# Two projection groups as one seven-product block multiplication, with weight sums made by accumulating DMAs

## The chip, the cores and the metric

The kernel runs on one core of a Trainium2 chip, as one program. The metric is device time in microseconds from launch to end, lower is better. The engines named here are TensorE (PE: matmuls; PEld is its weight load), VectorE (DVE), ScalarE (ACT), GpSimd (POOL) and SyncE (SP). SP does no arithmetic; its queue issues nearly all DMAs, in program order, and a DMA that has to wait there holds all that stand behind it. POOL issues the DMAs that add to their destination.

## What is computed

A decoder block over 1024 tokens of width 1024: an RMS norm with adaptive scale and shift gives `h`, one wide projection of `h` feeds a retention mixer and a dilated sliding-window attention in three groups of four heads, both are gated and merged, and a squared-ReLU MLP follows. The part that matters here is the projection, and of it the attention values of the three groups:

```python
proj = h @ w_in
parts = jnp.split(proj, IN_OFFSETS, axis=-1)
...
for gi, (win, dil) in enumerate(ATT_GROUPS):
    aq, ak, av = parts[4 + 3 * gi], parts[5 + 3 * gi], parts[6 + 3 * gi]
```

Each `av` is `h` (1024 x 1024) times a weight of 1024 x 512.

## The kernel before

All matmuls are made of three: an operand is split into a high part in the fast float32 format (`hi`, a cast on ACT) and a low part (`lo = x - hi`, a subtraction on DVE), and a product is lo x hi + hi x lo + hi x hi, accumulated in PSUM (`mm3`, L197). `h` lies in SBUF transposed, as eight pairs `hh[k]`, `hl[k]` of 128 channels by 1024 tokens. A matmul is 128 x 128 by 128 x 512; PSUM has eight banks of 128 x 512.

The order of the instructions on each engine is the order in which the program writes them; the program sets it by hand, and semaphores only make an engine wait. So an instruction that waits holds what is behind it on its engine. Tiles come from pools: `raw` (three slots, L144) for weights as loaded, `wh` and `wl` (three slots each) for their parts, and `x` (26 slots, `x4`, L332) for nearly all else in this stage. A new tile waits until the last reader of the tile that had its slot is done.

**Startup and the first value group** (`av_first`, L779). `h` is made channel block by channel block: DVE scales `xt[k]`, ACT makes `hh[k]`, DVE `hl[k]`. As soon as block k is there, PE multiplies it with the weight rows k of group 0 (`av_k`, L746), for eight token blocks at once, in eight banks. At k = 4 `bias_out` (L436) puts the attention bias into DRAM: three times one small write and four broadcast writes that wait for it. After k = 7 ACT copies the eight banks to SBUF tiles `avo`, and SP writes them to `va_d`.

**The second and the third group** (`av_step`, L854) go the same way, now with `h` complete: for each of the eight k and eight token blocks three matmuls, in all 2 x 8 x 8 x 3 = 384, and again eight copies and eight writes at the end of each group. The weights of a pair of k are one load of 128 x 1024; the planner `Steps` (L55) issues the loads as slots of `raw` come free, and splits a weight ahead of its step.

**Sums of h** (`sums_of_h`, L824). The stages that follow (queries, keys, gates, retention values) use Winograd's form of Strassen's algorithm: the tokens are cut in halves and the channels in even and odd blocks, and seven products of half size replace eight. Their left operands are blocks of `h` and the sums t1 to t4, each a set of four tiles `xat` (t4 takes the place of half of `hh` and `hl`, whose contents are saved to DRAM in `h12_d` before). In the kernel before t1, t3 and t2 are made within the second group, and t4 at the head of `queries_keys` (L954). One set is four times a DVE operation, a cast on ACT and a subtraction on DVE.

**Queries and keys** (`queries_keys`). The class `Blocks` (L220) runs the seven products for each pair of 128 output columns. Its `prep` makes the sums of the weights on DVE and splits them, some products ahead; `post` takes the banks out (L280 is a copy on ACT, L284 and L285 are subtractions on DVE). Four operands of the first pair are prepared within the third value group.

**Sums in DRAM.** For later stages, weight sums are made in DRAM: `copy_block` copies a block and `quarter_sums` (L548) adds others to it with DMAs that POOL issues (L552; L556 and L558 are plain copies among them), each of 512 KB. These begin with `queries_keys`. `VPLAN` lists the seven products of the retention values: which left operand, which sign of the weight, and which of three bank groups (a, b, c) they are accumulated in.

Of the kernel before, what the change touches and what calls it, by code (L numbers as in the profile page):

```python
# [11 lines left out]
F32 = mybir.dt.float32  # L12
F32R = mybir.dt.float32r
AF = mybir.ActivationFunctionType
# [120 lines left out]
def block_kernel(ctx, tc, io, stop=None, dbg=None):  # L135
# [3 lines left out]
    def fv(t):  # L139
        return t.bitcast(F32)  # L140
# [638 lines left out]
    def av_first(kk):  # L779

        def body(ahead, w):
            for k in (2 * kk, 2 * kk + 1):
                if k == 0:
                    for j, rb in enumerate(first["rb"]):
                        nc.scalar.copy(rb1[:, 512 * j:512 * j + 512], rb)
                if k % 2 == 0:
                    ahead(1)
                if k + 1 < NK:
                    h1_mods(k + 1)
                    h1_scale(k + 1)  # L790
# [24 lines left out]
        return body  # L815
# [35 lines left out]
            low = lo, r, hi  # L851
        nc.vector.tensor_sub(low[0], low[1], fv(low[2]))

    def av_step(g, kk):  # L854
        def body(w):
            if (g, kk) == (1, 0):
                for m in range(4):
                    nc.sync.dma_start(h12_d[m][:, 0], fv(hh[2 * m][:, 512:]))
                    nc.sync.dma_start(h12_d[m][:, 1], fv(hl[2 * m][:, 512:]))
                sh = mods[:, SH1:SH1 + NK].rearrange("p (m j) -> p m j", j=2)  # L860
                nc.vector.tensor_sub(dsh1, sh[:, :, 0], sh[:, :, 1])
            for k in (2 * kk, 2 * kk + 1):
                av_k(g, k, w)
            if g == 1 and kk < 3:
                sums_of_h(("t1", "t3", "t2")[kk])
            if (g, kk) == (1, 3):
                a_load(0, 1)
                a_load(0, 2)
            if (g, kk) == (2, 1):
                BA.prep((0, "11"), (0, "s1"))  # L870
            if (g, kk) == (2, 2):
                a_load(1, 1)
                a_load(1, 2)
                BA.prep((0, "s3"), (0, "s2"))
        return body
# [224 lines left out]

    for kk in range(4):
        steps.add(av_first(kk), [(io["w_av"][kk], split_first)], manual=True)
    for g in (1, 2):
        for kk in range(4):
            steps.add(av_step(g, kk), [(io["w_av"][4 * g + kk], split_first if (g, kk) == (1, 0) else split_w)])
    steps.mark()
    steps.add(queries_keys, manual=True)

    later_mods = [G1 + k for k in range(NK)] + [SH2 + k for k in range(NK)] + \
# [1343 lines left out]
```

## Time and profile before

| | us |
|---|---|
| three timed runs | 2242.38, 2243.01, 2244.39 (median 2243.01) |
| profiled execution, first to last instruction | 2248.9 |
| its mean granted TensorE clock | 0.993 of full |
| first matmul of the second value group | 72.50 |
| first matmul of queries and keys | 159.54 |

The profiled execution has no time of its own beside its span of 2248.9 us. All times below are from its start. A line of the page's or the trace's groups reads: program line, engine, operation, output <- inputs, shapes, count | busy time in us, mean ns of one | idle time of the engine before them and what ended it. A line in order of time reads: start, length, engine, line, operation, output <- inputs, count, and in square brackets the idle time before it and what released it. The table of stages gives for each stretch the busy time and the number of instructions of each engine, the granted clock, the share of time that the DMA engines were busy and GB/s. In the lists of DMAs the last number is the median time from issue to landing.

### The profile page before, as it was taken

How to read it: one execution, taken by the hardware profiler on the slowest of the kernel's cores; microseconds unless marked ns; L12 is line 12 of the kernel's file. 1: busy time of each engine (PE TensorE's matmuls, PEld its weight loads, DVE VectorE, ACT ScalarE, POOL GpSimd, SP SyncE). 2: the span in 40 equal slices, each digit the busy share in tenths (PEclk: the TensorE clock that was granted, in tenths of full speed). 3: DMA queues.
4: the chain of work that ended last, by engine and by line, in shares of the span. 5: the costliest groups of instructions: out<-in, count | busy, mean ns of one | idle time of the engine just before them, and what ended most of it. 6: DMA issues, size and time to landing. Idle time of an engine off the chain costs nothing.

```text
span 2248.9 us, 27131 instructions
## 1 busy us (share of the span) xinstructions
PE 2183.6 (97%) x10130; PEld 1808.0 (80%) x10130; DVE 1455.3 (65%) x2285; ACT 908.6 (40%) x1665; POOL 145.6 (6%) x168
## 2 busy tenths in 40 slices
PE   7999999999999999999999999999999999999998
PEld 5887888887877888887788788888778888888887
DVE  6527777753548778853554554576866665787845
ACT  4323333223334445534634633434454445533412
POOL 0001111000011122100000000002100000000003
PEclk9999999999999999999999999999999999999999
DMA  9648999625775556549723345645134443745322
GB/s 361 197 145 277 289 284 287 198 93 178 246 271 169 168 181 206 191 165 241 207 78 94 105 178 210 247 156 178 61 136 155 155 155 145 266 151 169 122 85 76
DMA packets 154371, 408.93 MB, mean 182 GB/s; under 512 B 27062, under 2 KB 54973, under 8 KB 149822
## 3 DMA queue, kind: packets, MB, share of 16 engines
q1 hardware_dynamic: 148542, 363.14, 46.3%
q0 software_dynamic: 5696, 44.04, 8.2%
q8 instruction: 80, 1.31, 0.2%
q14 instruction: 53, 0.43, 0.1%
HBM read 316.27 MB, written 156.13 MB: 210 GB/s over the span
## 4 chain that ended last, share of the span: by engine, by line
PE 47%; DVE 5%; ACT 2%; DMA 2%; issue 1%; SPq 0%; POOL 0%; POOLq 0%; DVEq 0%; ACTq 0%
PE fp L201 4%; PE fp L203 4%; PE fp L205 4%; PE f2a L203 2%; PE f2a L205 2%; PE f2a L201 2%; PE ak L201 1%; PE ak L203 1%; PE ak L205 1%; PE wo L201 1%; PE wo L205 1%; PE wo L203 1%; PE roa L203 1%; PE roa L201 1%; PE roa L205 1%
## 5 line engine op out<-in xcount | busy, mean ns | idle before, releaser
L201 PE MATMUL qap<-hh,qaw 128*128 128x512 f32 x216 | 84.3, 390 | 3.9 <-ACT qat L280 2.2
L205 PE MATMUL qap<-hh,qaw 128*128 128x512 f32 x216 | 84.1, 389 | 0.0
L203 PE MATMUL qap<-hl,qaw 128*128 128x512 f32 x216 | 84.0, 389 | 0.0
L614 POOL TENSOR_TENSOR j<-qk,j 128x512 fp32r<-128x512 f32 x32 | 43.4, 1356 | 470.2 <-ACT j L613 470.2
L1912 ACT ACTIVATE a<-a 128x512 f32<-128x512 f32 x48 | 30.3, 631 | 79.1 <-DVE a L1911 79.1
L1266 ACT ACTIVATE P<-P,ng 128x128 f32<-128x128 f32 (+1 forms) x96 | 41.9, 438 | 41.8 <-DVE ng L1263 41.8
L1809 POOL TENSOR_TENSOR accnf<-accnf,sqnf 128x256 f32<-128x256 f32 (+1 forms) x18 | 16.6, 922 | 619.0 <-ACT sqnf L1808 619.0
L258 DVE TENSOR_TENSOR fw<-w1r,fw 128x512 fp32r<-128x512 f32 x48 | 33.0, 688 | 36.3 <-ACT fw L248 36.3
L2098 ACT CAST w2h<-w2s 128x512 fp32r<-128x512 f32 x36 | 22.4, 621 | 77.6 <-DVE w2s L2136 75.3
L201 PEld LDWEIGHTS qap<-hh,qaw 128*128 128x128 f32 x216 | 40.5, 188 | 13.2 <-ACT qat L280 2.6
L201 PE MATMUL fp<-h2h,fw 128*128 128x512 f32 x128 | 50.0, 390 | 0.0
L203 PE MATMUL fp<-h2l,fw 128*128 128x512 f32 x128 | 49.8, 389 | 0.0
L205 PE MATMUL fp<-h2h,fw 128*128 128x512 f32 x128 | 49.8, 389 | 0.0
L201 PE MATMUL roa<-rh,rwl 128*128 128x512 f32 x128 | 49.8, 389 | 0.0
L203 PE MATMUL roa<-rl,rwh 128*128 128x512 f32 x128 | 49.8, 389 | 0.0
L205 PE MATMUL roa<-rh,rwh 128*128 128x512 f32 x128 | 49.8, 389 | 0.0
L636 ACT COPY sm<-sT 128x128 f32<-128x128 f32 x32 | 8.5, 267 | 101.8 <-PE sT L627 100.1
L1647 DVE TENSOR_TENSOR rwl<-rwl,rwh 128x1024 fp32r<-128x1024 f32 x25 | 30.2, 1221 | 29.0 <-ACT rwh L1677 29.0
L1809 POOL TENSOR_TENSOR accn<-accn,sqn 128x512 f32<-128x512 f32 x12 | 15.5, 1296 | 491.8 <-ACT sqn L1808 491.8
L205 PEld LDWEIGHTS qap<-hh,qaw 128*128 128x128 f32 x216 | 40.5, 188 | 8.4
L203 PEld LDWEIGHTS qap<-hl,qaw 128*128 128x128 f32 x216 | 40.5, 188 | 8.3
L1204 DVE SCALAR_TENSOR_TENSOR ql<-raw,qh 128x1024 fp32r<-128x1024 f32 x12 | 14.7, 1224 | 47.6 <-ACT qh L1203 47.6
(3081 smaller groups left out, 7216.7 us busy)
## 6 DMA issues: line engine op xcount, KB each, us to landing
v<-vd SPq DMA_DIRECT2D x32, 512.0 KB, 5.4
raw<-in_w_ada_dram SPq DMA_DIRECT2D x32, 512.0 KB, 4.9
w1r<-in_w_ff_dram SPq DMA_DIRECT2D x32, 512.0 KB, 5.1
vd<-vo SPq DMA_DIRECT2D x24, 512.0 KB, 6.4
yt<-y POOLq DMA_DIRECT2D x6, 2048.0 KB, 15.0
xsd<-as SPq DMA_DIRECT2D x24, 512.0 KB, 2.7
w2r<-in_w_ff2s_dram SPq DMA_DIRECT2D x24, 512.0 KB, 7.1
em<-in_w_ada_dram SPq DMA_DIRECT2D x16, 512.0 KB, 10.2
```

The lines of the kernel that those rows point to most:

```text
L201: nc.tensor.matmul(o, wl, xh, start=first, stop=False, skip_group_check=skip)
L203: nc.tensor.matmul(o, wh, xl, start=False, stop=False, skip_group_check=skip)
L205: nc.tensor.matmul(o, wh, xh, start=False, stop=last, skip_group_check=skip)
L258: nc.vector.tensor_sub(t[:, 512:], src, fv(t[:, :512]))
L614: nc.gpsimd.tensor_sub(t[:, 1], src, fv(t[:, 0]))
L636: nc.scalar.copy(sm, ps[:, :C])
L1204: nc.vector.scalar_tensor_tensor(lo, raw, QSCALE, fv(hi), op0=ALU.mult, op1=ALU.subtract)
L1266: nc.scalar.activation(v, v, AF.Exp, bias=ng[:, blk:blk + 1], accum_out=st[:, g, blk, 2 + a:3 + a])
L1647: nc.vector.tensor_sub(lo, fv(lo), fv(hi))
L1809: (nc.vector if f == 7 else nc.gpsimd).tensor_add(G["acc", key], G["acc", key], sq)
L1912: nc.scalar.activation(o, o, AF.Relu)
L2098: nc.scalar.copy(hi, src)
```

## The change

The second and third group together are `h` (1024 x 1024) times a weight of 1024 x 1024. The change makes this one block multiplication with seven products, by the plan `VPLAN`: blocks 11, 12, s1, s2, s3, 22, s4, each of four quarters m, four token blocks p and three matmuls, 48 in all, so 336 for the stage (`av_blocks`, `avb_mm`). The first digit of a weight block is the group, the second the parity of the channel block.

- *Weights.* The four loads of group 1 (`avb_load`: abr0 to abr3) serve blocks 11 and 12 together. They are issued on SP at k = 4 (abr0, behind `bias_out`), k = 5 (abr2), k = 6 (abr1) and after k = 7 (abr3, behind the writes of `avo`), and are split (`avb_split`) before k = 6 and before k = 7 (abr0, abr1) and after the first quarter of block 11 (abr2, abr3). The planner no longer loads these groups.
- *Sums of weights.* s1 = 21 + 22, s2 = s1 + 11 and s4 = s2 + 12 are made one after the other in the same two `raw` tiles: a load by SP, then DMAs of POOL that add from DRAM into SBUF, the next one issued as soon as the tile has been split (`avb_sum`). s3 = 21 + 11 is a load and one addition in `x` tiles, 22 a plain load (`avb_fetch`). Each has two halves j; each addition moves 512 KB in rows of 2 KB. That is eight accumulating DMAs.
- *Banks.* `avb_post` takes a block's banks out during the first quarter of the next: blocks 11, s2, s1 and 22 by ACT, 12, s3 and s4 by an addition or subtraction on DVE. The results go to `va_d` as before.
- *Sums of h.* t1 is made after k = 7, behind the copies of the first group; t3 after the second quarter of block 11, t2 after the third of block 12, t4 after the second of s1. `queries_keys` no longer makes t4. The saves to `h12_d` move ahead of the loads of cos, sin and decay.
- *Operands of the first pair of queries and keys* are loaded in block s2 and prepared in blocks s3 and 22.

```diff
+                if k in (6, 7):
+                    avb_split(k - 6)
                 av_k(0, k, w)
...
                 if k == 4:
                     for g in range(3):
                         bias_out(g)
+                    avb_load(0)
+                if k == 5:
+                    avb_load(2)
+                if k == 6:
+                    avb_load(1)
+                    for j in range(2):
+                        avb_sum(j, "s1")
                 if k == NK - 1:
-                    ahead(1)
-                    if first["lows"]:
-                        first["lows"].pop(0)()
+                    avb_load(3)
+                    for m in range(4):
+                        nc.sync.dma_start(h12_d[m][:, 0], fv(hh[2 * m][:, 512:]))
+                        nc.sync.dma_start(h12_d[m][:, 1], fv(hl[2 * m][:, 512:]))
+                    sh = mods[:, SH1:SH1 + NK].rearrange("p (m j) -> p m j", j=2)
+                    nc.vector.tensor_sub(dsh1, sh[:, :, 0], sh[:, :, 1])
+                    sums_of_h("t1")
                     nc.sync.dma_start(cs, io["cossin"])
                     nc.sync.dma_start(decay, io["decay"])
...
+    def avb_tile(n, part, name):
+        if n in (2, 6) or n > 11:
+            return x4(name, F32R)
+        return whl.tile([P, 1024], F32R, tag="w" + part, name=name)
+
+    def avb_load(m):
+        AB["w", m] = x4(f"abr{m}")
+        nc.sync.dma_start(AB["w", m], ABW[4 + m])
+
+    def avb_add(t, blk, j):
+        nc.gpsimd.dma_start(t, avb_src(blk, j), accum_op=ALU.add)
+
+    def avb_sum(j, n):
+        if n == "s1":
+            AB["s", j] = wraw.tile([P, 1024], F32, tag="raw", name=f"abs{j}")
+            nc.sync.dma_start(pairs_of(AB["s", j]), avb_src("21", j))
+        avb_add(pairs_of(AB["s", j]), {"s1": "22", "s2": "11", "s4": "12"}[n], j)
+
+    def avb_fetch(i, j):
+        n = ABSEQ[i]
+        raw = AB["w", i, j] = x4(f"abr{n}{j}")
+        nc.sync.dma_start(pairs_of(raw), avb_src("21" if n == "s3" else "22", j))
+        if n == "s3":
+            avb_add(pairs_of(raw), "11", j)
+
+    def avb_split(m, j=None):
...
+        hi, lo = avb_tile(n, "h", f"abh{n}"), avb_tile(n, "l", f"abl{n}")
+        nc.scalar.activation(hi, raw, AF.Copy, scale=sign)
+        if sign > 0:
+            nc.vector.tensor_sub(lo, raw, fv(hi))
+        else:
+            nc.vector.scalar_tensor_tensor(lo, raw, -1.0, fv(hi), op0=ALU.mult, op1=ALU.subtract)
+        AB["o", n] = hi, lo
+        if j is not None and ABSEQ[m] in ("s1", "s2"):
+            avb_sum(j, {"s1": "s2", "s2": "s4"}[ABSEQ[m]])
...
+        for p in range(4):
+            if m == 0 and i > 0:
+                avb_post(i - 1, p)
+            if new and m == 0:
+                AB["ps", bank, p] = ps_s(f"av{bank}{p}")
+            xh, xl = (z[:, p * P:p * P + P] for z in XA[x, m])
+            mm3([AB["ps", bank, p]], (xh, xl), [(wh, wl)], new and m == 0, m == 3, True)
...
+    def av_blocks(ahead):
+        work = {(0, 0): [lambda: avb_split(2), lambda: avb_split(3)],
+                (0, 1): [lambda: sums_of_h("t3")],
+                (1, 0): [lambda: avb_split(2, 0)], (1, 1): [lambda: avb_split(2, 1)],
+                (1, 2): [lambda: sums_of_h("t2")],
+                (2, 0): [lambda: avb_split(3, 0), lambda: avb_split(3, 1)],
+                (2, 1): [lambda: sums_of_h("t4")],
+                (2, 2): [lambda: avb_fetch(4, 0)], (2, 3): [lambda: avb_fetch(4, 1)],
+                (3, 1): [lambda: avb_fetch(5, 0), lambda: avb_split(4, 0)],
+                (3, 2): [lambda: avb_split(4, 1), lambda: a_load(0, 1)],
+                (3, 3): [lambda: a_load(0, 2)],
+                (4, 0): [lambda: avb_fetch(5, 1)],
+                (4, 1): [lambda: avb_split(5, 0)],
+                (4, 2): [lambda: avb_split(5, 1), lambda: BA.prep((0, "11"))],
+                (4, 3): [lambda: BA.prep((0, "s1"))],
+                (5, 0): [lambda: avb_split(6, 0)], (5, 1): [lambda: avb_split(6, 1)],
+                (5, 2): [lambda: a_load(1, 1), lambda: a_load(1, 2), lambda: BA.prep((0, "s3"))],
+                (5, 3): [lambda: BA.prep((0, "s2"))]}
+        for i in range(len(ABSEQ)):
+            for m in range(4):
+                avb_mm(i, m)
+                for f in work.get((i, m), ()):
+                    f()
...
     def queries_keys(ahead):
-        sums_of_h("t4")
```

More of the change, by code (lines that the diff above doesn't have):

```diff
@@ L852, in sums_of_h @@
         nc.vector.tensor_sub(low[0], low[1], fv(low[2]))
[L854 to L875, printed above, removed]
+    AB = {}
@@ new lines, in avb_add @@
+    def avb_add(t, blk, j):
[5 more added lines that the diff above has]
+        avb_add(pairs_of(AB["s", j]), {"s1": "22", "s2": "11", "s4": "12"}[n], j)
+    ABSEQ = ("11", "12", "s1", "s2", "s3", "22", "s4")
+    def avb_fetch(i, j):
[4 more added lines that the diff above has]
+            avb_add(pairs_of(raw), "11", j)
@@ new lines, in avb_mm @@
+    def avb_mm(i, m):
+        n = ABSEQ[i]
+        x, _, bank = VPLAN[n]
+        new = n in ("11", "12", "s1")
+        if i < 2:
+            t, c = AB["o", m], 512 * i
+        else:
+            t, c = AB["o", 2 * i + m // 2], 512 * (m % 2)
+        wh, wl = (z[:, c:c + 512] for z in t)
+        for p in range(4):
[5 more added lines that the diff above has]
+            mm3([AB["ps", bank, p]], (xh, xl), [(wh, wl)], new and m == 0, m == 3, True)
@@ new lines, in av_blocks @@
+    def av_blocks(ahead):
[21 more added lines that the diff above has]
+                    f()
+        for p in range(4):
+            avb_post(len(ABSEQ) - 1, p)
@@ L1102, in block_kernel @@
         steps.add(av_first(kk), [(io["w_av"][kk], split_first)], manual=True)
-    for g in (1, 2):
-        for kk in range(4):
-            steps.add(av_step(g, kk), [(io["w_av"][4 * g + kk], split_first if (g, kk) == (1, 0) else split_w)])
     steps.mark()
+    steps.add(av_blocks, manual=True)
     steps.add(queries_keys, manual=True)
```

35 lines of the change are left out of this document (added).

## The prediction

> **What bounds the kernel now.** I read the page first, then the table of stages around the change, then the queues in it.
>
> ```profile
> span 2248.9 us, 27131 instructions
> PE 2183.6 (97%) x10130; PEld 1808.0 (80%) x10130; DVE 1455.3 (65%) x2285; ACT 908.6 (40%) x1665; POOL 145.6 (6%) x168
> ```
>
> TensorE (PE) is busy from end to end: a matmul removed is worth its pace, and a wait of PE costs its length. The stages, with length, then busy time and count of each engine, granted clock, DMA share and GB/s:
>
> ```profile
> 72.50:83.40 10.90, 10.90 (x50) 9.03 (x49) 7.13 (x11) 6.97 (x12) 0.00 (x0) 1.00 0.92 275
> 83.40:105.00 21.60, 21.60 (x97) 17.90 (x96) 13.24 (x19) 7.09 (x10) 0.00 (x0) 1.00 0.73 275
> 127.00:148.00 21.00, 21.00 (x95) 17.38 (x94) 6.25 (x9) 3.44 (x5) 0.00 (x0) 1.00 0.00 0
> 170.00:180.00 10.00, 6.08 (x26) 4.38 (x25) 8.42 (x14) 4.51 (x9) 0.53 (x1) 1.00 1.03 279
> ```
>
> Through the second and third value group PE never waits, while VectorE (DVE), ScalarE (ACT) and the DMAs have room. PE waits only behind them, where queries and keys begin. The first matmul of the second group, the first of queries and keys, and PE's waits there:
>
> ```profile
> 72.50 0.39 PE L761 MATMUL av<-raw_530l,hh 128*128 128x512 f32 x1
> 159.54 0.39 PE L201 MATMUL qap<-hh,qaw 128*128 128x512 f32 x1
> ...
> PE qap L201 <- ACT qat L280: 2.2, 1, 2.2
> PE qap L201 <- DVE qat L285: 1.7, 1, 1.7
> ```
>
> **Removed.** The two groups are 2 x 8 x 8 x 3 = 384 matmuls in 159.54 - 72.50 = 87.0 us, so 0.2267 us each (the 0.39 is the length of one in the pipeline). The change needs 7 blocks x 4 x 4 x 3 = 336. **Term 1: 48 x 0.2267 = -10.9 us**, and a block is 48 matmuls, 10.9 us, in four quarters of 2.72.
>
> The sums t4 leave the head of queries and keys, where DVE and ACT work them off before anything else (some 5.3 us of DVE, by the rows of t1 below). The two waits above are of the copy L280 and the subtraction L285, which stand behind that work in their queues. With it done one block earlier both find their inputs in time. **Term 2: -3.9 us**; at worst 0, if DVE comes late out of the last block.
>
> **The start of the first block.** The new weight loads are on SP's queue behind the twelve writes of the bias, and ACT's copies that empty the eight banks of the first group are now behind the casts of two of these loads. SP's and ACT's rows:
>
> ```profile
> 41.05 14.25 SPq L85 DMA_DIRECT2D raw<-in_w_av_dram  x4
> 55.35 0.39 SPq L438 DMA_DIRECT2D browd<-rows  x1
> 58.90 2.49 SPq L441 DMA_DIRECT2D biasd<-browd  x4
> 71.53 2.39 SPq L441 DMA_DIRECT2D biasd<-browd  x4
> 74.90 5.92 SPq L768 DMA_DIRECT2D vad<-avo  x8
> ...
> 51.85 1.05 ACT L773 CAST raw_528h<-raw 128x1024 fp32r<-128x1024 f32 x1 [2.15 <-DMA raw<-in_w_av_dram]
> 71.11 4.01 ACT L767 COPY avo<-av 128x512 f32<-128x512 f32 x8 [4.38 <-PE av L761]
> ...
> DMA to landing us min/median/max: 5.6/8.8/10.7
> ```
>
> Before, the bias writes wait for four weight loads (41.05 to 55.3); after, only for the first of these, and start at some 41.4. Their first DMA still lies behind that load in the rings, which lands at 51.85; I let `biasd` begin at 53. From its first issue to the end of the third set is 71.53 + 2.39 - 58.90 = 15.0 us, each set waiting for a landing. So SP comes to abr0, abr2 and abr1, in this order, from 68.0 on. The last row is that of the loads of w_av; I take 7 us between its least and its median, as three 512 KB loads follow each other: abr1 is there at 76.0, cast at 77.1, and the emptying begins then, not at 71.11. PE starts when the first bank is empty, 77.6, not 72.5. **Term 3: +5.1** (2 with the least landing and a quicker bias chain, 9 with 10.7 us).
>
> **Third quarter of block 11.** Behind the eight copies ACT and DVE have the sums t1, and only then the split of abr2. The sums of h before, and a split:
>
> ```profile
> 78.44 1.29 DVE L834 TENSOR_TENSOR xt<-xt 128x512 f32<-128x512 f32 x2
> 83.01 0.69 DVE L852 TENSOR_TENSOR xat<-xt,xat 128x512 fp32r<-128x512 f32 x1
> 96.73 1.41 DVE L840 SCALAR_TENSOR_TENSOR xt<-xt,mods,xt 128x512 f32<-128x512 f32 x2
> 101.48 0.69 DVE L852 TENSOR_TENSOR xat<-xt,xat 128x512 fp32r<-128x512 f32 x1
> 106.47 1.22 DVE L192 TENSOR_TENSOR raw_708l<-raw,raw_708h 128x1024 fp32r<-128x1024 f32 x1 [4.30 <-ACT raw_708h L191]
> ```
>
> One set takes 5.3 us (78.44 to 83.70). Two subtractions run ahead of ACT; the rest starts when ACT has emptied the banks, 77.1 + 4.0 = 81.1, and ends at about 86 on DVE, 85 on ACT. The cast of abr2 is done at 86, its low part at 87.2. PE, at full pace, wants it after two quarters, at 77.6 + 5.4 = 83.0. **Term 4: +4.1** (3 to 5; all of it is order of queues).
>
> **Fourth quarter.** abr3 is issued behind the eight `vad` writes, which follow the copies: 77.6 + 5.9 = 83.5. With 6.5 us to landing it is there at 90.0, split at 92.2; PE wants it at 87.1 + 2.7 = 89.8. **Term 5: +2.4** (1.5 at 5.6 us, 6.5 at 10.7).
>
> **Block s1.** The split of s1 takes a `wh` slot that PE frees only within block 12 (after its first and second quarter). So DVE has, in order: low part of the second half at 5.4 + 1.05 + 1.22 + 0.2 = 7.9 us into block 12, the sums t2 (5.4 us, 96.73 to 102.17), then the four additions with which block 12's banks come free, and s1's new banks are those. The first addition, of a kind with this one,
>
> ```profile
> L924 DVE TENSOR_TENSOR qa<-qat,qap 128x512 f32<-128x512 f32 x22 | 16.7, 759 | 0.4
> ```
>
> ends at 7.9 + 5.4 + 0.76 = 14.1 us, and block 12 at 10.9. **Term 6: +3.2** (2 to 4).
>
> **The clock.** Waits of this size make matmuls slow afterwards:
>
> ```profile
> 507.20:509.20 2.00, 0.00 (x0) 0.00 (x0) 2.00 (x3) 0.00 (x0) 0.00 (x0) 0.98 0.31 123
> 509.20:512.60 3.40, 3.36 (x8) 2.71 (x9) 1.13 (x1) 0.00 (x0) 0.00 (x0) 0.51 1.03 318
> 1062.00:1070.40 8.40, 1.82 (x10) 1.24 (x10) 2.51 (x3) 3.24 (x4) 0.52 (x1) 0.91 1.04 334
> 1070.40:1077.00 6.60, 6.59 (x18) 5.24 (x19) 6.60 (x9) 0.82 (x1) 0.45 (x1) 0.60 0.62 181
> ```
>
> After 2 us without a matmul the granted clock was 0.51 for 3.4 us, after 6.6 us 0.60 for 6.6. At half clock 3.4 us of matmuls lose 1.7. After term 3 this costs nothing more, since PE would wait for abr2 anyway; after term 5 likewise, since block s1 waits for DVE's chain and not for PE; after term 6 nothing hides it. The stretch 170 to 180 has waits of 2.2 and 1.7 at clock 1.00, so the loss isn't sure; I take it. **Term 7: +1.6** (0 to 3.4). The Trainium skill, TensorE: Matmul & The Clock Gate, Part 1, says that the clock is halved after an idle window of about 3.4 us. By that alone the 3.2 us would be just too short, and the sum lower by 1.6; the 2 us row differs from it, and I go by the row.
>
> **The accumulating DMAs.** Eight, issued by GpSimd (POOL), which is idle here. Nothing before adds into SBUF; the nearest rows add DRAM to DRAM:
>
> ```profile
> 166.85 0.99 POOL L552 DMA_DIRECT2D wrvs<-in_w_rv_dram  x1 [147.45 <-DMA wrvs<-in_w_rv_dram]
> 177.26 0.53 POOL L556 DMA_DIRECT2D wrvs<-wrvs  x1 [8.28 <-DMA wrvs<-in_w_rv_dram]
> wrvs<-in_w_rv_dram POOLq DMA_DIRECT2D x16, 512.0 KB, 9.7
> L552 POOL DMA_DIRECT2D wros<-in_w_ret_out_dram x16: 772/852/1370, 296.8 to 425.6; - x16
> DMA to landing us min/median/max: 5.3/9.8/17.7
> ```
>
> Issue is 0.8 to 1.4 us each on a free engine: nothing. Landing is some 8.3 (a wait) to 9.7 us (a median on busy DMAs). s1 and s4 have over 15 us. s2 is added 8 us before the end of block 12 and read by block s2, 14 us later with term 6: it fits. The tight one is s3. Counted from the start of block s1: DVE's four additions end at 2.3, SP has put out four results at 3, then the load of block 21 (7 us), the addition (8.3), the other half 1.3 later, ACT's cast (1.05), and behind it on ACT the copy that frees bank a (0.6): 21.3. PE wants the bank at 21.8, or 23.4 with term 7. **Term 8: 0.** With the medians, 8.8 and 9.7, it is 24.5, a wait of 1; the worst landings make 11. ACT's queue is what then holds PE, for the cast that waits for the DMA stands ahead of the bank's copy. The Trainium skill, DMA: Bandwidth & Descriptors, Anatomy of one DMA, fits 2.0 us + bytes/436e3 to such a DMA; by that 512 KB would take an estimated 3.2 us and s3 could not be late. The rows show over twice that, so I keep the chance.
>
> **Edits at nothing.** Splits become 14 instead of 8 (6 x 1.22 us more DVE, 6 x 1.05 more ACT); ACT keeps 16 copies of banks and DVE gets 12 additions (9.1 us). With t3, t2, t4 and the operands of the first product (some 5) DVE comes to 14 x 1.22 + 3 x 5.3 + 9.1 + 5 = 47 of 76 us, and ACT to less. PE's blocks hide all of it but at the places above; without that cover the six splits and the additions would be 16 us of DVE. The `h12` saves on SP now stand ahead of cos and sin, first read after the first pair of queries and keys: nothing. All later work shifts as a whole.
>
> **Sum:** -10.9 - 3.9 + 5.1 + 4.1 + 2.4 + 3.2 + 1.6 + 0 = +1.6 us on the profiled execution's 2248.9, +0.07%. The median of the runs is 2243.0, 5.9 below that span; on it the forecast is **2244.6 us**. Measurement tells about 0.2%, 4.5 us, from no change, so this is "same".
>
> **Rivals.**
> (a) Faster. The first block isn't held: abr0 and abr1 land before ACT comes to empty the banks. This needs abr1 5 us sooner than I reckon, so that term 3 falls to at most 1, and abr3, which follows, costs 0. Then -14.8 + 1 + 4.1 + 3.2 = -6.5, 2236.5. For it: the DMA share falls after the startup loads. Against it: the 15.0 us of the bias chain, which are waits for landings, not bandwidth. It decides if abr1 lands by 72. Chance 0.2.
> (b) Slower through s3: additions into SBUF in 2 KB rows land after 15 us rather than 8.3. Then s3's chain is 28 against 23.4, term 8 is 4.6, PE's clock falls once more (1.7), and the time is 2244.6 + 6.3 = 2251. For it: no row shows this kind, and the DRAM kind reached 17.7 at worst. Against it: the DMAs have little else then (0.00 share at 127 to 148). It decides when load and addition together take over 20 us, instead of 15.3. Chance 0.2.
> (c) The matmuls go but the time doesn't: the landings of terms 3 and 5 are near their maxima, or the slot of abr3 comes free only when a `vad` write has landed: +4 on each, 2249 to 2253. Chance 0.15.
>
> **How the numbers follow.** The forecast has 0.45; its own range, from terms 3 to 7 partly at their ends, is 2240 to 2249. With (a) down to 2237 and (b) and (c) up to 2254 the range holds 8 in 10. Faster 0.2 is (a); slower 0.35 is (b) and (c); same 0.45.
>
> **What would show it.** 336 matmuls at 0.227 us; the emptying of the first group (71.11 before) at 75 to 79 behind a cast that waits for a DMA; PE waiting for the low part of abr2, then of abr3; PE waiting for DVE's addition at the start of block s1, with the clock at half afterwards; no wait for the copy and the subtraction at the head of queries and keys. The prediction is wrong if PE goes into block 11 at 73, if block s3 waits for its addition, or if other waits than these make up the sum.

## The result and the profile after

| | before | after |
|---|---|---|
| median of the runs, us | 2242.7 (2241.69 to 2244.39, 4 runs) | 2258.07 (2256.57 to 2258.95, 4 runs) |
| profiled execution, first to last instruction | 2248.9 | 2257.2 |
| its mean granted TensorE clock | 0.993 | 0.989 |

The changed kernel is slower: ratio 1.0067, 95% interval 1.0052 to 1.0081, or 15.4 us between the medians. That is beyond the upper end of the predicted range, 2254. The page of the kernel after, its span and the busy time of each engine:

```profile
span 2257.2 us, 27110 instructions
PE 2177.6 (96%) x10082; PEld 1801.3 (80%) x10082; DVE 1470.3 (65%) x2303; ACT 912.2 (40%) x1671; POOL 155.3 (7%) x176
```

The 48 matmuls have gone (10130 to 10082), and POOL has eight instructions more, the additions. What PE waits for in the stage of the change (engine, tile and line, what it waited for, then us in total, times, the longest):

```profile
PE ava L201 <- ACT abr L951: 12.6, 1, 12.6
PE ava L201 <- ACT avo L767: 6.0, 1, 6.0
PE avc L201 <- DVE abr L957: 3.1, 1, 3.1
PE ava L203 <- DVE abl L919: 1.5, 2, 0.8
PE ava L201 <- ACT abh L917: 1.4, 2, 0.9
```

Before, there was no wait in the second and third group, and two at the head of queries and keys, which are gone. The first matmuls of the blocks 11, 12, s1, s2, s3 and s4, of queries and keys, and of the stage behind them (`va`), in order of time in the kernel after, and the last of these in the kernel before:

```profile
78.47 0.80 PE L201 MATMUL ava<-abh,hl 128*128 128x512 f32 x1 [6.01 <-ACT avo L767]
95.39 0.39 PE L201 MATMUL avb<-abh,hl 128*128 128x512 f32 x1
109.54 0.66 PE L201 MATMUL avc<-abh,xat 128*128 128x512 f32 x1 [3.11 <-DVE abr L957]
122.13 0.39 PE L201 MATMUL ava<-abh,xat 128*128 128x512 f32 x1
145.79 0.80 PE L201 MATMUL ava<-abh,xat 128*128 128x512 f32 x1 [12.62 <-ACT abr L951]
169.94 0.39 PE L201 MATMUL avc<-abh,hl 128*128 128x512 f32 x1
180.82 0.39 PE L201 MATMUL qap<-hh,qaw 128*128 128x512 f32 x1
523.54 0.39 PE L201 MATMUL va<-vwh,hl 128*128 128x512 f32 x1
```

```profile
506.79 0.39 PE L201 MATMUL va<-vwh,hl 128*128 128x512 f32 x1
```

A block at full pace is 10.9 us. So each step of this list over 10.9 is a loss in its block, and the list is an account of the whole stage: it ends at 180.82 instead of 159.54, 21.3 us later, and queries and keys then give 4.5 back (523.54 - 506.79 = 16.75). Four stretches of the kernel after (length; busy time and count on PE, PEld, DVE, ACT, POOL; granted clock, DMA share, GB/s):

```profile
78.40:81.00 2.60, 2.53 (x6) 2.04 (x7) 2.08 (x4) 2.60 (x7) 1.38 (x1) 0.50 0.70 254
111.00:112.00 1.00, 1.00 (x4) 0.81 (x3) 1.00 (x2) 0.00 (x0) 0.00 (x0) 0.50 1.12 180
133.50:146.00 12.50, 0.21 (x1) 0.21 (x2) 1.93 (x2) 2.85 (x4) 1.22 (x1) 0.64 0.51 84
145.70:149.00 3.30, 3.21 (x8) 2.54 (x9) 1.64 (x2) 2.46 (x5) 0.00 (x0) 0.50 0.00 0
```

PE stands still for 12.6 us ahead of block s3 while the DMA engines are half idle (0.51), and behind each of the three long waits its clock is 0.50 for some microseconds. Who is late there is seen on POOL, which issues the additions (two to each of s2, s4 and s3, in this order), and on ACT, which casts s3's weights and behind them copies the bank that block s3 needs. Both in order of time, in brackets the idle time before and what ended it; last, from issue to landing of s3's two additions:

```profile
101.86 1.21 POOL L889 DMA_DIRECT2D abs<-in_w_av_dram  x1 [13.48 <-DVE abl L919]
108.10 1.23 POOL L889 DMA_DIRECT2D abs<-in_w_av_dram  x1 [5.03 <-DVE xat L861]
114.61 1.21 POOL L889 DMA_DIRECT2D abs<-in_w_av_dram  x1 [5.28 <-DMA abs<-in_w_av_dram]
125.67 1.22 POOL L889 DMA_DIRECT2D abs<-in_w_av_dram  x1 [9.85 <-issue]
132.03 1.21 POOL L889 DMA_DIRECT2D abrs<-in_w_av_dram  x1 [5.14 <-issue]
138.19 1.22 POOL L889 DMA_DIRECT2D abrs<-in_w_av_dram  x1 [4.94 <-issue]
...
137.96 1.06 ACT L917 ACTIVATE abh<-abrs 128x1024 fp32r<-128x1024 f32 x1 [14.68 <-DMA abrs<-in_w_av_dram]
144.21 1.06 ACT L917 ACTIVATE abh<-abrs 128x1024 fp32r<-128x1024 f32 x1 [5.20 <-DMA abrs<-in_w_av_dram]
145.17 2.03 ACT L951 COPY abr<-ava 128x512 f32<-128x512 f32 x4
...
DMA to landing us min/median/max: 5.8/5.9/5.9
```

An addition takes 1.2 us of POOL and lands in some 6 (5.8 to 6.2; only the first of s4, beside loads of SP, in 10.7). But the next is not issued for 5 us more, three times with nothing named that it waits for ("issue"): from start to start it is 6.2 to 6.5 us, a landing and some 0.3. The additions go one at a time. Those of s3, needed first, stand behind s4's, of which the second had itself waited 9.85 us for the landing of the first. ACT's copies, ready long before, stand behind the cast that waits for the last landing.

### The profile page after: what moved, and what is told of

The parts are those of the page before. It is cut to its first block, busy times and chain, and to the rows that moved or that the text cites. A ratio compares the mean times of both kernels' runs of the same rounds, so it can differ in the third digit from the quotient of the medians.

```text
span 2257.2 us, 27110 instructions
## 1 busy us (share of the span) xinstructions
PE 2177.6 (96%) x10082; PEld 1801.3 (80%) x10082; DVE 1470.3 (65%) x2303; ACT 912.2 (40%) x1671; POOL 155.3 (7%) x176
## 4 chain that ended last, share of the span: by engine, by line
PE 84%; DVE 5%; DMA 4%; issue 3%; ACT 2%; SPq 1%; POOL 0%; POOLq 0%; DVEq 0%; ACTq 0%
PE qap L203 5%; PE qap L205 5%; PE qap L201 5%; PE fp L201 4%; PE fp L203 4%; PE fp L205 4%; PE rg L201 3%; PE rg L203 3%; PE rg L205 3%; PE f2a L203 2%; PE f2a L205 2%; PE f2a L201 2%; PE ak L201 2%; PE ak L203 2%; PE ak L205 2%
## 5 line engine op out<-in xcount | busy, mean ns | idle before, releaser
L258 DVE TENSOR_TENSOR qaw<-wa,qaw 128x512 fp32r<-128x512 f32 x54 | 37.0, 686 | 6.9 <-ACT qaw L248 6.9
```

The costliest lines, as they stand in the source:

```text
L258: nc.vector.tensor_sub(t[:, 512:], src, fv(t[:, :512]))
```

## The experiments

The theory: the additions are a line on POOL, one in flight at a time, and the order in that line is not the order of use; the wait ahead of block s3 follows from both. Rivals: the additions themselves are slow (short rows, read and write of SBUF), whatever the order; or the earlier waits of the stage push everything and the wait at s3 is their sequel. Differences between versions are between medians; the median of the kernel before was 2242.4 to 2243.5 us in the groups of runs below. A trace is one execution, and from the first matmul of `va` to the end the traces of these versions take 1730.6 to 1741.3 us; so a version is also compared by the time at which queries and keys, or `va`, begin.

**More room for descriptors on POOL.**

```diff
-    nc = _bacc.Bacc("TRN2", target_bir_lowering=False, num_devices=1, dynamic_dma_scratch_size=1024)
+    nc = _bacc.Bacc("TRN2", target_bir_lowering=False, num_devices=1, dynamic_dma_scratch_size=4096)
```

> The changed kernel with four times the room for the descriptors that GpSimd writes (4096 instead of 1024), nothing else changed. Theory: the wait of 12.6 us in block s3 comes from the additions standing in line, because GpSimd cannot write the descriptors of the next 256-row addition before the last one has landed (5 us of 'issue' wait ahead of each, 6.2 us from one to the next). Then those gaps go, s3's two halves land by about 130 instead of 144, PE's wait in block s3 falls below 2 us, its half-clock stretch goes, and the time is 2242 to 2246. Rival: the additions wait for their data or for one another, whatever the room; then the gaps stay at 5 us, the wait at 12 to 13 us and the time at 2258.

Measured: 2252.19 us (2250.29 to 2257.5), ratio to the kernel before 1.0049 (1.003 to 1.0067), 6 us better than the change, and not the 2242 to 2246 that I expected. The profiled execution is the slowest of the four (2257.5). PE's waits for s3 and in block 11, POOL's rows and the landings of s3's pair; then the stage in which they lie:

```profile
PE ava L201 <- ACT abh L917: 4.1, 2, 3.5
PE ava L201 <- ACT abr L951: 1.4, 1, 1.4
...
117.06 2.44 POOL L889 DMA_DIRECT2D abs<-in_w_av_dram  x2 [7.77 <-DVE abl L921]
121.14 2.46 POOL L889 DMA_DIRECT2D abrs<-in_w_av_dram  x2 [1.64 <-DMA abrs<-in_w_av_dram]
...
DMA to landing us min/median/max: 14.8/15.5/16.3
```

```profile
123.00:136.00 13.00, 13.00 (x59) 10.78 (x58) 0.24 (x1) 2.39 (x4) 0.59 (x1) 1.00 1.09 262
```

A pair is now issued back to back (x2 in 2.44 us): the 5 us between two were for want of room. The wait at s3 falls from 12.6 to 1.4. But the first matmul of queries and keys is still 13.4 us later than before: in block 11 a wait of 3.5 us for the cast of abr3 takes part of its place. abr3's load, with both additions of s1 in flight beside it, is cast 9.3 us after its issue, against 6.7 in the change. And four in flight take 12 to 16 us each: they, with the loads beside them, now fill the DMA engines (1.09, against 0.51). So the room is one half of the answer; s4's pair, not needed yet, shares the engines with s3's, and the order is tried next.

**The order alone: s4's additions behind s3's.**

```diff
-        if j is not None and ABSEQ[m] in ("s1", "s2"):
-            avb_sum(j, {"s1": "s2", "s2": "s4"}[ABSEQ[m]])
+        if j is not None and ABSEQ[m] == "s1":
+            avb_sum(j, "s2")
...
-                (2, 2): [lambda: avb_fetch(4, 0)], (2, 3): [lambda: avb_fetch(4, 1)],
+                (2, 2): [lambda: avb_fetch(4, 0)], (2, 3): [lambda: avb_fetch(4, 1), lambda: avb_sum(0, "s4"), lambda: avb_sum(1, "s4")],
```

> The changed kernel with the two additions of s4, which are read only in the last block, put behind the two of s3 on GpSimd. Theory (additions in line, 6.2 us each): s3's halves are added at about 121 and 127 instead of 132 and 138 and land at 127 and 133; PE's wait in block s3 falls from 12.6 to 0 to 2 us, the time to 2242 to 2246. Rival (an addition into SBUF is slow while SP's loads run, whatever its place): s3 still lands after 140, time 2256 to 2258.

Measured: 2249.59 us (2249.19 to 2253.84), ratio 1.0036 (1.0023 to 1.005), 8.5 us better than the change, but short of the 2242 to 2246 expected. POOL's rows of s3, and PE's wait ahead of block s3:

```profile
121.52 1.21 POOL L889 DMA_DIRECT2D abrs<-in_w_av_dram  x1 [10.15 <-DVE xt L856]
130.66 1.22 POOL L889 DMA_DIRECT2D abrs<-in_w_av_dram  x1 [7.92 <-issue]
```

```profile
PE ava L201 <- ACT abr L951: 2.1, 1, 2.1
```

With the room as it was, the order alone takes the wait from 12.6 to 2.1. The additions still go one at a time. Either remedy alone takes most of the wait away, so it needed both: the line and the wrong order in it. The time stays above before because the other waits of the stage are still there (7.0 ahead of block 11, 3.1 ahead of s1).

**The earlier waits: bias writes behind the first group.** This takes the wait ahead of block 11 away without touching the additions.

```diff
                 if k == 4:
-                    for g in range(3):
-                        bias_out(g)
                     avb_load(0)
...
                     nc.sync.dma_start(decay, io["decay"])
+                    for g in range(3):
+                        bias_out(g)
```

> The changed kernel with the bias writes moved behind everything else that the first group issues on SP, so that the weight loads do not wait for them. Theory of term 3: PE's wait of 6.0 us ahead of block 11 falls under 1, the half-clock stretch behind it goes, the third quarter of block 11 then shows its wait in full (about 3 us), and everything behind comes 5 to 6 us earlier, time 2252 to 2253. Rival: the queue is not what holds these loads, but the DMA rings are still full of the startup loads; then the wait stays above 4 and the time at 2257 to 2258.

Measured: 2253.2 us (2252.97 to 2262.28), ratio 1.0059 (1.0038 to 1.0079). The bank copies of the first group start at 72.0 instead of 77.85 and the wait of 6.0 is gone. But PE comes earlier to a line that has not moved as much:

```profile
PE ava L201 <- ACT abr L951: 17.1, 1, 17.1
```

The wait at s3 grows from 12.6 to 17.1, for the last addition is issued only 2 us sooner (136.12 instead of 138.19). Of 6 us saved early 2.8 are left where queries and keys begin. The wait at s3 isn't a sequel of the early ones: it swallows part of what mending them gains. The medians differ by more, 4.9 us; the rest lies behind `va`, where it may be scatter, and was not traced.

**Longer rows.** The weights of these groups laid out so that an addition has 128 rows of 4 KB.

```diff
-        t = ABW[4 * int(blk[0]) + 2 * j:4 * int(blk[0]) + 2 * j + 2]
-        return t[:, :, 512 * (int(blk[1]) - 1):512 * int(blk[1])].rearrange("m p c -> p m c")
+        return io["w_avb"][2 * int(blk[0]) + int(blk[1]) - 3, j].rearrange("p (m c) -> p m c", m=1)
...
-        return t.rearrange("p (m c) -> p m c", m=2)
+        return t.rearrange("p (m c) -> p m c", m=1)
...
+    a["w_avb"] = np.ascontiguousarray(a["w_av"][4:].reshape(2, 2, 2, P, 2, 512).transpose(0, 4, 1, 3, 2, 5)).reshape(4, 2, P, 1024)
```

> The changed kernel with the weight blocks laid out in DRAM so that each load and addition has 128 rows of 4 KB instead of 256 of 2 KB; same bytes. Theory (the descriptors are what fills the room): two or more additions go out one after the other without the 5 us wait, and the block s3 wait falls by at least 6 us, time 2244 to 2252. Rival (bytes or the landing count): 6 us from one addition to the next as before, time 2256 to 2258.

Measured: 2250.93 us (2247.97 to 2258.88), ratio 1.0043 (1.0029 to 1.0057). With half as many rows, two or three additions are in flight in the same room, and issue is shorter (0.87 us instead of 1.2). s3's second still waits on POOL (start, length, idle before):

```profile
128.75 0.88 POOL L888 DMA_DIRECT2D abrs<-in_w_avb_dram  x1 [6.44 <-issue]
```

The wait at s3 is 2.0, with the DMA engines nearly full as in the first run (0.95 from 118.0 to 138.9). Together with that run this says that short rows act through the number of rows that the room holds. That longer rows would also move faster isn't seen: the last four additions, issued from 118.0, are only all in when s3's second cast begins, at 138.9, some 5 us for each.

**Without the additions.** The eight are left out, so that all four sums are block 21 alone.

```diff
     def avb_add(t, blk, j):
-        nc.gpsimd.dma_start(t, avb_src(blk, j), accum_op=ALU.add)
+        pass
```

> The changed kernel with the eight adding DMAs left out, so that s1, s2, s3 and s4 are all block 21 alone and the values of the second and third group come out other than the reference's; loads, splits, products and all else stay. Theory: the additions cost PE the wait in block s3 and the half-clock stretch behind it, 12.6 + 3.5 us, and nothing else; the other waits (6, 1.3, 1.7 and 3.1 us) stay, and the time is 2258 - 16 = 2242, queries and keys begin 16 us sooner than in the changed kernel. Rival: half of it is the load of s3 behind other loads on SP, or ACT's queue; then a wait of over 4 us stays in block s3 and the time is 2247 or more.

Measured: 2239.95 us (2238.29 to 2244.44), ratio 0.9992 (0.9983 to 1.0001): no change from before, and 18 us under the change. Its waits of over 1 us ahead of the blocks, with none at s3:

```profile
PE ava L201 <- ACT avo L767: 5.3, 1, 5.3
PE avc L201 <- DVE abr L957: 3.1, 1, 3.1
```

The additions are worth the whole loss: `va` begins at 506.72, against 523.54 in the change and 506.79 before. What remains is the sum of the prediction's other terms, +1.6 by its reckoning, -0.1 in this trace up to `va`, and -2.6 between the medians of this group of runs. Not all of the loss lies at s3. Block 11 takes 14.69 us here (77.75 to 92.44) instead of 16.92: abr3's load, which in the change has the first additions of s1 beside it, is issued at 82.24 and cast at 87.16, instead of 83.73 and 90.39.

**The kernel before again.** The profiled execution of before has a wait of 6.6 us at the gate products, at 1064 to 1070, which the change doesn't touch.

> The kernel before once more, for a second trace. The first shows PE waiting 6.6 us at 1064 to 1070 for a split weight, with the clock at half behind it, where the changed kernel shows 0; the timed runs of before are 6 us shorter than that profiled execution. If the wait belongs to that one execution, it is gone or smaller here and the span is 2240 to 2244; if it belongs to the kernel, it is there again with a span of 2249.

Measured: 2244.86 us in one run, a span of 2243.0, and no such wait; the gate products begin 4.5 us earlier than in the first profile. So that wait, with the half clock behind it, belongs to one execution. It accounts for most of why the two profiled spans differ by 8.3 us and the runs by 15.4 (against this second span it is 14.2); the accounts here are taken ahead of that place.

**All queues reordered.** Weight loads ahead of the bias writes; t1, t3 and t2 behind the splits and bank additions that they held; s3 loaded and added early, ahead of s2 and s4.

```diff
                 if k == 4:
-                    for g in range(3):
-                        bias_out(g)
                     avb_load(0)
+                    avb_load(1)
                 if k == 5:
                     avb_load(2)
+                    avb_load(3)
                 if k == 6:
-                    avb_load(1)
                     for j in range(2):
                         avb_sum(j, "s1")
+                    for g in range(3):
+                        bias_out(g)
                 if k == NK - 1:
-                    avb_load(3)
...
-                    sums_of_h("t1")
...
-                (0, 1): [lambda: sums_of_h("t3")],
-                (1, 0): [lambda: avb_split(2, 0)], (1, 1): [lambda: avb_split(2, 1)],
-                (1, 2): [lambda: sums_of_h("t2")],
-                (2, 0): [lambda: avb_split(3, 0), lambda: avb_split(3, 1)],
-                (2, 1): [lambda: sums_of_h("t4")],
-                (2, 2): [lambda: avb_fetch(4, 0)], (2, 3): [lambda: avb_fetch(4, 1)],
-                (3, 1): [lambda: avb_fetch(5, 0), lambda: avb_split(4, 0)],
+                (0, 1): [lambda: sums_of_h("t1"), lambda: avb_fetch(4, 0)], (0, 2): [lambda: avb_fetch(4, 1)],
+                (1, 0): [lambda: sums_of_h("t3")],
+                (1, 1): [lambda: avb_split(2, 0), lambda: avb_split(2, 1)],
+                (2, 0): [lambda: sums_of_h("t2"), lambda: avb_split(3, 0)], (2, 1): [lambda: avb_split(3, 1)],
+                (3, 0): [lambda: sums_of_h("t4"), lambda: avb_split(4, 0)],
+                (3, 1): [lambda: avb_fetch(5, 0)],
```

> The seven products with another order around them: all weight loads ahead of the bias writes, t1 behind the splits of abr2 and abr3, t3 and t2 behind the copies and additions that free banks, and s3 loaded and added in block 11, ahead of s2 and s4. By the terms: 3, 4, 5 and 6 go to 0 to 1 us each, 7 and 8 to 0, and what is left is -10.9 and -4 us: 2227 to 2232, faster than the kernel before. Rival: the additions (6.2 us each, two of s3 now ahead of s2's) make block s2 wait instead, 5 us or more, and the time is 2236 or more.

Measured: 2248.21 us (2245.67 to 2251.86), ratio 1.0026 (1.0016 to 1.0035). The waits of 6.0 and 3.1 and those of block 11 are gone, so the order of these queues was their cause; which move took which wait away was tried singly only for the bias writes. One new wait stands in their place, ahead of block s2. It, and POOL's rows for s3's two and then s2's first:

```profile
PE ava L201 <- ACT abh L916: 16.9, 1, 16.9
```

```profile
99.33 1.21 POOL L888 DMA_DIRECT2D abrs<-in_w_av_dram  x1 [30.16 <-DMA abrs<-in_w_av_dram]
109.24 1.23 POOL L888 DMA_DIRECT2D abrs<-in_w_av_dram  x1 [8.69 <-issue]
115.39 1.21 POOL L888 DMA_DIRECT2D abs<-in_w_av_dram  x1 [4.93 <-issue]
```

POOL waits 30 us for the load that its addition adds to, which SP issues late (91.4), behind the bias, the results of the first group, the saves of `h` and the loads of cos, sin and decay. The additions of s2, which could go, stand behind it. I had put the wrong pair in front.

**The same with the room at 4096.**

> The reordered kernel with room for 4096 descriptors. If the order has taken the additions off the path, the room changes nothing: within 3 us of e7. If they still hold a block, this is faster by the part that the gaps of 5 us make, 3 us or more.

Measured: 2239.5 us (2237.86 to 2241.78), ratio 0.9987 (0.9978 to 0.9996), with a wait of 11.8 us ahead of block s2. The room helps by 9 us, more than the 3 us at which I would have called the additions still on the path, and the wrong order still costs.

**The additions in the order of use, s1, s2, s3, s4**, with the room as it was and at 4096.

```diff
-                (0, 1): [lambda: sums_of_h("t1"), lambda: avb_fetch(4, 0)], (0, 2): [lambda: avb_fetch(4, 1)],
+                (0, 1): [lambda: sums_of_h("t1")],
...
+                (1, 2): [lambda: avb_fetch(4, 0), lambda: avb_fetch(4, 1)],
```

> As e7_reordered, with one thing moved: the loads and additions of block s3 are asked for behind the split of block s1, so that on GpSimd the additions stand in the order of use, s1, s2, s3, s4. Theory (the additions are a line, some 6.2 us from one to the next, and the one that is needed next must stand first): block s2's additions are issued near 91 and 97 and have landed by about 103, block s2 begins near 110, so its wait of 16.9 us goes to under 1; block s3's follow at 102 to 109 and land by 115, block s3 begins near 122, no wait; the first matmul of the gate products is some 13 us ahead of e7's and the time is 2230 to 2237. Rival (the additions, and the loads of 512 KB around them, need the DMA engines for longer than the stage has, in any order): the wait only moves to block s3 or s4, 5 to 12 us of it are left, and the time is 2241 to 2248.

> As e9_s2first, with the room for GpSimd's descriptors at 4096 instead of 1024, so that both additions of a pair are issued at once. Theory of the line: with the order right there is slack of several us ahead of each block, so this is within 3 us of e9, 2229 to 2237, and the waits of blocks s2 and s3 are under 1 us in both. Rival (the room is what counts, not the order): e9 keeps a wait of 5 us or more that this kernel hasn't, and is slower than it by 6 to 10 us.

Measured: 2240.77 us (2237.01 to 2249.52), ratio 0.9989 (0.9977 to 1.0001), at the small room, and 2232.17 us (2230.48 to 2237.58), ratio 0.9955 (0.9942 to 0.9969), at the large one. At the small room the order takes 16.9 us of wait to 2.6 in s2 and 6.3 at s3, so the first was as its rival had it, in the wait that is left and nearly in time; the second differs from it by 8.6 us, as the rival of the room had it, though a wait of 5.0 us at s3 is left in it too. What still waits at the small room, and ACT's rows there:

```profile
PE ava L201 <- ACT abr L950: 6.3, 1, 6.3
113.26 0.50 PE L201 MATMUL ava<-abh,xat 128*128 128x512 f32 x1 [2.59 <-ACT abh L916]
```

```profile
112.15 1.06 ACT L916 ACTIVATE abh<-abs 128x1024 fp32r<-128x1024 f32 x1 [8.41 <-DMA abs<-in_w_av_dram]
113.11 2.04 ACT L953 ACTIVATE abr<-avc 128x512 f32<-128x512 f32 x4
...
126.45 1.06 ACT L916 ACTIVATE abh<-abrs 128x1024 fp32r<-128x1024 f32 x1 [6.39 <-DMA abrs<-in_w_av_dram]
127.41 2.03 ACT L950 COPY abr<-ava 128x512 f32<-128x512 f32 x4
```

The bank copies at 113.11 and 127.41 are issued at once behind a cast that has waited for a landing. It is the cast of a second half, which its block needs only in its third quarter. The copy at 127.41 is what block s3 waits 6.3 us for. The wait of 2.6 is another kind: block s2 began at 105.07, PE stands at its third quarter, and it waits for the late cast itself.

**Those casts behind the bank copies**, again at both rooms.

```diff
-                (2, 0): [lambda: sums_of_h("t2"), lambda: avb_split(3, 0)], (2, 1): [lambda: avb_split(3, 1)],
-                (3, 0): [lambda: sums_of_h("t4"), lambda: avb_split(4, 0)],
+                (2, 0): [lambda: sums_of_h("t2"), lambda: avb_split(3, 0)],
+                (3, 0): [lambda: avb_split(3, 1), lambda: sums_of_h("t4"), lambda: avb_split(4, 0)],
...
-                (3, 2): [lambda: avb_split(4, 1), lambda: a_load(0, 1)],
+                (3, 2): [lambda: a_load(0, 1)],
...
-                (4, 0): [lambda: avb_fetch(5, 1)],
+                (4, 0): [lambda: avb_split(4, 1), lambda: avb_fetch(5, 1)],
```

> As e9_s2first, with the casts of the second half of block s2's and block s3's weights behind the bank copies that they held up on ScalarE (behind the first quarter of their own blocks; a block needs its second half only in its third quarter). Theory (what is left of the wait is ScalarE's order: a cast that waits for a landing stands ahead of the bank copies that the next block waits for): in e9 the copies came at 113.1 and 127.4, right behind casts at 112.2 and 126.5; without that the waits of 2.6 and 6.3 us go to under 1, blocks s2 and s3 begin near 110 and 123, their third quarters near 116 and 129, after the halves have landed, and with the room of 1024 the time is 2229 to 2235, 6 to 11 us under e9. Rival (the landings themselves are late, and the wait only moves from the block's head to its third quarter): the third quarter of block s3 waits 3 us or more, and the time is within 4 us of e9's.

> As e11_cast_late, with the room for GpSimd's descriptors at 4096. Theory of ScalarE's order: the wait of 5.0 us at block s3 goes too, the blocks run without a wait over 0.5 us, and the time is 2224 to 2229, 4 to 8 us under e10. Rival (half clock: what the wait cost is only its 5 us, or the throttle takes something back elsewhere in the stage): 2229 to 2232.

Measured: 2232.35 us (2231.14 to 2238.85), ratio 0.9962 (0.9949 to 0.9975), at the small room, 8.4 us under the run before it (`va` begins 9.4 us earlier, at 496.02), as the theory had it: the wait of 6.3 is 0.5 now. In block s2 1.6 of the 2.6 is left, for that half still lands late. At the large room 2235.15 us (2231.48 to 2238.43), ratio 0.9963 (0.995 to 0.9977): no gain on 2232.17, not the 2224 to 2229 of the theory and above the 2229 to 2232 of its rival. In the profiles of both, queries and keys begin earlier than in the best run above (153.31 and 152.72 against 155.83), but 500 us later there is a longer wait at the retention's gate. PE's row there in the kernel at the small room:

```profile
659.76 1.22 PE L201 MATMUL rg<-hh,raw_4653l 128*128 128x512 f32 x2 [8.26 <-DVE kl L647]
```

At the large room it is 9.1 us, in the slowest of the five executions; in the change and all its other versions it is 3.3, in the two traces of the kernel before 4.6 and 5.9. The trace puts ACT's copy ahead of it down to the landing of a store of retention values. Whether that store is late for reasons of its own, or because of the earlier start, was not tried. So once the order of both queues is right, POOL's and ACT's, the room makes no difference that these runs show. The best two versions, one with a wait of 5.0 us at s3 and the other with 8.3 at the gate, reach 2232, 0.4% under the kernel before; a version without either was not found.

## Why the prediction was wrong, point by point

The sum failed in one step, term 8. The measured terms come from the list of first matmuls, each block against 10.88 us, and add up to the 16.75 us by which `va` begins later. The runs differ by 15.4; the wait at the retention's gate is shorter in the change, 3.3 against 4.6 and 5.9.

| step | predicted | measured, us |
|---|---|---|
| 1, 48 matmuls | -10.9 | -10.9 |
| 2, head of queries and keys | -3.9 | -4.5 (342.72 instead of 347.25 to `va`) |
| 3, start of block 11 | +5.1 | +6.0 (78.47 - 72.50) |
| 4 and 5, its third and fourth quarter | +6.5 | +6.0 (block 11 takes 16.92) |
| 6, ahead of block s1 | +3.2 | +3.3 (block 12 takes 14.15) |
| 7, half clock behind it | +1.6 | +1.7 (block s1 takes 12.59) |
| 8, the additions | 0 | +12.8 ahead of s3 (23.66), +2.4 half clock (24.15 for two blocks) |

- **Terms 1 to 7** came out as reasoned, within 1 us each (4 and 5 together). In terms 4 and 5 there was some luck: in the trace without the additions block 11 loses 3.8 us and not 6.0, and the prediction had put the additions at nothing there too. The casts that hold ACT's bank copies stand where they were put, at 74.30 and 76.89, and the copies start at 77.85 (77.1 predicted):

```profile
74.30 1.06 ACT L917 ACTIVATE abh<-abr 128x1024 fp32r<-128x1024 f32 x1 [7.78 <-DMA abr<-in_w_av_dram]
76.89 1.06 ACT L917 ACTIVATE abh<-abr 128x1024 fp32r<-128x1024 f32 x1 [1.53 <-DMA abr<-in_w_av_dram]
77.85 3.99 ACT L767 COPY avo<-av 128x512 f32<-128x512 f32 x8
```

  In block 11 the waits shown are short (twice 0.76, 0.54 and 0.90), because PE came through its first half at a clock of 0.50 to begin with and was late itself. As the prediction said, that cost nothing more: the cast of abr2 was the end that counted.
- **Term 7 and the clock.** Behind a wait of 3.11 us the clock was 0.50 (111 to 112), and block s1 lost 1.7 us. The Trainium skill, TensorE: Matmul & The Clock Gate, Part 1, gives an idle window of about 3.4 us for this and calls the window free-running. The run shows that 3.1 us is enough here (the trace models where a matmul ends; from the start of the last one ahead of the wait to the start of the first behind it are 3.50 us). The row of 2 us that the term went by is a weaker ground than it looked: the same wait of 2.07 us stands in all 14 traces, and the clock of the 2 us behind it was 0.50 to 0.83 in six of them and 1.00 in eight. The waits of 3.1 us ahead of s1, in six traces, all have 0.50 to 0.53 behind them.
- **Term 8, the step that failed:** "Issue is 0.8 to 1.4 us each on a free engine: nothing", and for s3 "the other half 1.3 later". POOL is busy only 1.2 us with an addition, as said, but it could not issue the next until the last had landed, 6.2 us from start to start. I looked for the cost in the landing, which is shorter than I took (5.9, not 8.3), and not in the issue. The nearest rows gave no warning: before, three DRAM-to-DRAM additions of 512 KB go out in 2.40 us, at 0.8 us of issue each, near the 0.87 of the additions with longer rows. Whether their rows or their destination makes the difference was not tried. And I counted s3's chain as if it began on an empty POOL, though the diff has s4's additions, called at the split of s2, ahead of it. The prediction did name what then holds PE: "the cast that waits for the DMA stands ahead of the bank's copy". That is the wait of 12.6 us. The three additions in the kernel before:

```profile
232.29 2.40 POOL L552 DMA_DIRECT2D wrvs<-in_w_rv_dram  x3 [6.16 <-DMA wrvs<-wrvs]
```

- **Rival (b)** named the place and the price's kind, s3 late and the clock halved once more, with 2251. Its mechanism, slow landings, is not what happened in the kernel after. It did happen with four in flight (12 to 16 us each), and there s3's wait was 1.4. **Rival (a)** fell: nothing in block 11 went faster. Its sum also leaves out term 7, which by the prediction's own words nothing hides; with it the time would be 2238.1, not 2236.5. **Rival (c)** fell too: term 3 is 6.0, and terms 4 and 5 together 6.0, near what was reckoned and not 4 us over each.
- The Trainium skill, DMA: Bandwidth & Descriptors, Anatomy of one DMA, fits 2.0 us + bytes/436e3, an estimated 3.2 us for 512 KB, and says that many descriptors can be emitted before their cost shows. The run shows 5.8 to 6.2 us for an addition into SBUF that is alone in flight, longer than the fit, and 5 us of waiting on POOL between two additions of 256 rows each, at which its sentence on descriptors doesn't hint. Both differ in the direction that makes the change slower.

## What to carry to other kernels

An engine that is shown idle is not thereby free to issue: before many DMAs are put on one queue that has carried few, take its spacing from start to start, not its busy time, and write down the queue's order against the order of use. A cast that waits for a DMA belongs behind every copy on its engine that frees a bank, if its operand isn't needed sooner; here that alone was worth 8 us at the small room, and nothing that the runs show at the large one. And when several waits follow one another, the last one can hide part of the gain of mending the first.

## What the runs showed of the hardware

- POOL's accumulating DMAs of 256 rows of 2 KB went one at a time with the program's descriptor room of 1024: next issue some 0.3 us after the landing, 6.2 us from start to start for s3's. With 4096, or with 128 rows of 4 KB, two and more were in flight.
- One at a time, the DMA engines were busy for 0.51 of the time at 84 GB/s; four in flight, with loads beside them, took 12 to 16 us each at a share of 1.09 and 262 GB/s. More room shortens the line, but each addition then takes longer to land.
- The clock was 0.50 behind waits of PE of 3.1, 6.0 and 12.6 us. Behind the shortest and the longest the blocks lost 1.7 and 2.4 us: far from proportional to the wait. In the six traces with 3.1 us of wait block s1 lost 1.5 to 3.0. A wait of 2.07 us, the same in all 14 traces, was followed by a lowered clock in six.
